# Attention rows kept as two half-precision planes, turned by transposing loads ahead of the output projection, in a hybrid decoder layer on one core

## The chip, the cores and the metric

One NeuronCore of one Trainium2 chip runs the whole kernel. The metric is device time of one execution in microseconds (us). The kernel before took 1151.21 us, median of 3 runs (1151.15 to 1152.17).

## The reference, cut to what matters

One decoder layer of width 1024 on a sequence of 2048 rows, batch 1, all inputs float32. `FOX` is causal softmax attention with a forget-gate bias (8 heads of 64), `SWA` is attention in a sliding window of 128 keys with rotary positions and a learned sink (8 query heads, 2 key/value heads).

```python
mod = silu(c) @ w_ada + b_ada                       # shift, scale, gate: 1024 each
h = rms_norm(x, g_pre) * (1 + scale) + shift
qa, ka, va, fa, za, qb, kb, vb, zb = split(h @ w_in)
oa = forgetting_attention(qa, ka, va, fa + b_fgate) * silu(za)      # [2048, 512]
ob = sliding_window_sink_attention(rope(qb), rope(kb), vb, sinks) * silu(zb)   # [2048, 512]
y = concatenate([oa, ob], axis=-1) @ w_out          # [2048, 1024] @ [1024, 1024]
out = x + gate * rms_norm(y, g_post)
```

## The kernel before, in words

**Numbers.** TensorE works on float16 pairs: a float32 value times a power of two is kept as a high part (a copy to float16) and a low part (value minus high part). A product of two such pairs is three float16 matmuls: high by high, high by low, low by high.

**Stages.** The work is one long program in a hand-written order for all engines (`tc.manual_schedule()`). First the input is normalised, turned and projected. Then come 32 `Pair` windows of the sliding-window attention, with projections filled in between (`fill`). Then comes the forgetting attention: 8 heads `hd`, each of 20 `Step`s `r` (two key blocks against a chunk `ci` of 512 queries, 4 chunks per head, with 2, 4, 6 and 8 steps). Last comes the output projection, class `Out`, one object for each of 16 tiles `t` of 128 rows. The first units of it are filled into the last head.

**Where attention rows go.** Both attentions write their divided results to DRAM, in `o_d`, four tensors of 512 rows by 1024 columns in float32. A window does it in `out_` (line 934): VectorE multiplies by the inverse sums into the tile `on`, and GpSimd's queue issues the store (line 938). A head's chunk does it at the end of `Step.pv` (line 1363): VectorE writes `ona`, and SyncE's queue (SP) issues the store (line 1368). The gates, silu paths already in transposed layout, are written to `z_d`, with the feature on the partition.

**The output projection, tile by tile.** `load_z` and `load_o` (lines 1454 and 1459) bring a tile's gates and its 128 rows of `o_d` into two buffers each, cut from `Ts[0]`. `turn` (line 1465) transposes the rows on TensorE: 8 float32 transposes of 128 by 128 against the identity (line 1469) into two PSUM banks. Later steps of it are put off by ticks (`after(n, f)` calls `f` at the n-th next `tick()`): `gate` multiplies the banks with the gates (line 1478, VectorE, twice 512 columns), `squares_` sums squares (1481, ScalarE), `scale_` adds over partitions with a matmul (1485) and makes a power-like scale, then the high part (1491, ScalarE) and the low part (1492, VectorE) go to the tile `oz`. `product(n, k)` (line 1494) issues three matmuls of 512 columns (line 1505) for feature block `k` and output half `n`; a tile has 16 such units, 48 matmuls. After the eighth unit `evac` squares the bank (1513, ScalarE) and multiplies by the gate vector (1521, VectorE). `root` is a chain of small VectorE operations (lines 1531 to 1552), and `store` (1555) adds the residual (1559, VectorE) and issues the output store on SP's queue (1560).

**Order.** `ofill` runs the units in order: tiles 0 and 1 interleaved, then tile after tile, with a `tick` every second unit. Tile t + 1 is turned after the third unit of tile t, with its scale 4 ticks later. In the last head (`hd == 7`) tiles 0 and 1 are loaded at steps 4 and 6 and turned at 6 and 8; the last 16 projection units lie in steps 0 to 7, and 33 units of the output projection in steps 10 to 19. `w_out_load` and `w_out_split` bring and split the output weights in the same head.

**Buffers.** `op_` (tags `tz`, `ona`) has two buffers in the forgetting attention, `onp` two. Gates' small tiles (`nn`, `cm`, `tot`) lie in the pool `fap`.

Of the kernel before, what the change touches and what calls it, by code (L numbers as in the profile page):

```python
# [18 lines left out]
P = 128  # L19
S = 2048  # L20
D = 1024
# [19 lines left out]
def hybrid_layer(  # L41
# [32 lines left out]

    o_d = [dram.tile([CH, D], F32, name=f"o_d{t}") for t in range(NCH)]
    z_d = dram.tile([KT, P, S], F32, name="z_d")
# [111 lines left out]
    def after(n, f):  # L188
        late.append([n, f])
# [610 lines left out]
    def gates():  # L800

        nn = fap.tile([P, 2, NB, 8], F32, tag="nn", name="nn")
        nf, na = nn[:, 0], nn[:, 1]
# [10 lines left out]
        def sums():  # L814
# [3 lines left out]
            PE.matmul(pc[:, P:2 * P], ones[:], lsf, start=True, stop=True)  # L818
            cm = fap.tile([P, 2, NB, 8], F32, tag="cm", name="cm")
            V.tensor_copy(cm[:].rearrange("p a t h -> p (a t h)"), pc[:, 0:2 * P])  # L820
# [5 lines left out]
            for r in (2, 3):  # L826
                V.tensor_tensor(inn[:, :, r, :], inn[:, :, r - 1, :], blk[:, :, r - 1, :], op=ALU.add)
            tot = fap.tile([P, 4, 8], F32, name="tot")
# [5 lines left out]
            V.tensor_tensor(csum[:].rearrange("p h t -> p t h"), cm[:, 0], na,  # L834
                            op=ALU.add)

        after(1, logs)
# [11 lines left out]
    class Pair:  # L849
# [73 lines left out]
        def pv(self):  # L923
# [10 lines left out]
            def out_():  # L934
                on = onp.tile([P, 2, P], F32, tag="on", name="on")
                V.tensor_tensor(on[:].rearrange("p e (h d) -> p (e h) d", h=2), po[:],
                                self.rinv[:].unsqueeze(2).broadcast_to([P, 4, 64]), op=ALU.mult)
                G.dma_start(o_d[i // 4][(i % 4) * P:(i % 4 + 2) * P, (4 + j) * P:(5 + j) * P]
                            .rearrange("(e p) c -> p e c", p=P), on[:])

# [164 lines left out]
    with swa_order:  # L1105
# [47 lines left out]
        windows[NW - 1].pv()  # L1153
        tick()
        tick()
        banded[0] = False
# [15 lines left out]
    foxl, foxo = ExitStack(), ExitStack()  # L1172
    op_ = foxl.enter_context(tc.tile_pool(name="opa", bufs=2, reuse_waits="tile"))
    stp = foxl.enter_context(tc.tile_pool(name="stpa", bufs=3, reuse_waits="tile"))
# [139 lines left out]
    class Step:  # L1314
# [35 lines left out]
        def pv(self):  # L1350
# [12 lines left out]
            if self.last:  # L1363
                rinv = sm(4, "a_ri")
                V.reciprocal(rinv[:], po[:, :, 64])
                on = op_.tile([P, 4, 64], F32, tag="ona", name="ona")
                V.tensor_tensor(on[:], po[:, :, 0:64], rinv[:].unsqueeze(2).broadcast_to([P, 4, 64]), op=ALU.mult)  # L1367
                SP.dma_start(o_d[self.ci][:, hd * 64:(hd + 1) * 64].rearrange("(u p) d -> p u d", p=P), on[:])

# [25 lines left out]
    def open_out():  # L1395
# [3 lines left out]
        wo = foxo.enter_context(tc.tile_pool(name="wo", bufs=1, reuse_waits="tile"))  # L1399
        op_ = foxo.enter_context(tc.tile_pool(name="opo", bufs=2, reuse_waits="tile"))  # L1400
        stp = foxo.enter_context(tc.tile_pool(name="stpo", bufs=4, reuse_waits="tile"))
# [14 lines left out]
        spare = hT[2][:].rearrange("p a k n -> p (a k n)")  # L1416
        oio["r"] = [spare[:, 2 * CH * n:2 * CH * (n + 1)].bitcast(F32) for n in range(6)]
        oio["j"] = [spare[:, CH * a:CH * b].bitcast(BF16) for a, b in ((12, 14), (14, 15), (15, 16))]
        rotate("x", oxy[:2])
# [22 lines left out]
    class Out:  # L1442


        def __init__(self, t):
            self.t = t
            self.last = t == NB - 1
            self.cuts = (0, CH, CH + 3 * P, D) if self.last else (0, CH, D)

        def load(self):  # L1450
            self.load_z()
            self.load_o()
# [12 lines left out]
        def turn(self, lag):  # L1465

            px = [bk[bank()][:].rearrange("p (k n) -> p k n", k=4) for _ in range(2)]
            for k in range(KT):
                PE.transpose(px[k // 4][:, k % 4, :], self.o[:, k * P:(k + 1) * P], ident[:])  # L1469
# [3 lines left out]
            gs = sm(1, "w_mx")  # L1473

            def gate():
                for h in range(2):
                    z = self.z[:, 4 * h:4 * h + 4, :]
                    V.tensor_tensor(z, px[h], z, op=ALU.mult)  # L1478

# [12 lines left out]
            after(lag + 2, lambda: V.scalar_tensor_tensor(lo, self.z, self.sc[:], hi, op0=ALU.mult, op1=ALU.subtract))  # L1492

        def product(self, n, k):
# [15 lines left out]
            def evac():  # L1510
                if n == 0:
                    self.y = oio["y"]()
                A.activation(oio["j"][1 + n % 2][:, :cc.stop - cc.start], py, AF.Square, accum_out=self.ss[:, n:n + 1])
                if self.last:
                    if n == 0:
# [47 lines left out]

    ounits, oloads = [], {}
    for t, n in [(0, 0), (1, 0), (0, 1), (1, 1)] + [(t, n) for t in range(2, NB) for n in range(len(outs[t].cuts) - 1)]:
        if n == 0 and t + 2 < NB:
            oloads[len(ounits)] = t + 2
        for q in range(KT):
            ounits.append(lambda t=t, n=n, q=q: outs[t].product(n, q))
            nxt = 2 if (t, n) == (0, 1) else t + 1 if n == 0 and 2 <= t < NB - 1 else None  # L1570
            if q == 2 and nxt:
                ounits.append(lambda nxt=nxt: outs[nxt].turn(4))
    opos = [0]
    N_IN = 4 * KT + 1

    def ofill(n, each=None):
        for _ in range(n):
            if opos[0] in oloads:
                outs[oloads[opos[0]]].load()
            ounits[opos[0]]()  # L1580
            opos[0] += 1
            if each:
                each()

    with tc.manual_schedule():
# [29 lines left out]
        for s, stp_ in enumerate(steps):  # L1615
# [116 lines left out]
```

## Time and profile before

| | |
|---|---|
| median of the runs | 1151.21 us |
| the profiled execution's own time | 1151.65 us |
| its span, first to last instruction | 1149.9 us |
| outside the span | 1.75 us |
| mean granted TensorE clock | 0.998 of full speed |
| busy: TensorE, VectorE, ScalarE, GpSimd | 97%, 79%, 59%, 15% of the span |
| DMA moved | 136.36 MB, 119 GB/s mean |
| `o_d` loads in the output projection | 16 of 512 KB |
| `o_d` stores | 64 of 128 KB, half by GpSimd's queue, half by SP's |

Engines: PE is TensorE's matmul, PEld its weight loads, DVE VectorE, ACT ScalarE, POOL GpSimd, SP SyncE. A name with a small q (SPq) is that engine's instruction queue: issue of DMAs and waits on semaphores. A row of the windows view has the stretch in us, its length, then the busy time of each engine with its count of instructions, then the granted clock, the mean busy share of the 16 DMA engines (it can pass 1, since packets of one engine overlap) and what they moved in GB/s. A row of the chain has start, duration, engine, tile and line. A row of the view of one line has engine, operation, count, then duration in ns as smallest/median/largest, and the first and last start.

### The profile page before, as it was taken

The numbers are of one execution on the slowest core, as the hardware profiler recorded it, in microseconds if no ns is written. First come the engines' busy times: TensorE is split into PE (matmuls) and PEld (weight loads), VectorE is DVE, ScalarE is ACT, GpSimd is POOL, SyncE is SP. The second block draws the span as 40 slices with busy tenths as digits, with TensorE's granted clock in tenths as the row PEclk, the third lists the DMA queues.
The fourth block names the chain that finished last, engine by engine and source line by source line (L and its number), as shares of the span: only waits on it lengthen the run. The fifth ranks groups of instructions, "written<-read, shape, count | busy, mean of one in ns | idle before, by whom it ended". The sixth has DMA issues, their size and how long they took to land. (4 is left out here: it accounts for less than half of the span.)

```text
span 1149.9 us, 27039 instructions
## 1 busy us (share of the span) xinstructions
PE 1112.5 (97%) x10514; PEld 650.9 (57%) x10514; DVE 907.7 (79%) x2330; ACT 678.4 (59%) x1124; POOL 169.5 (15%) x302
## 2 busy tenths in 40 slices
PE   5899999999999999999999999999999989999997
PEld 1466657655579865555555555555555555455553
DVE  6776668879888577889988989888898886766666
ACT  4676446556566525766767667667777698233331
POOL 2011122333322201112111111111010010000000
PEclk9999999999999999999999999999999999999999
DMA  9646426687777423333333232214121264464542
GB/s 327 225 139 170 106 70 139 112 170 139 176 143 128 97 61 84 81 86 74 84 81 97 64 86 68 62 38 100 45 56 34 66 195 145 163 207 166 201 169 88
DMA packets 162452, 136.36 MB, mean 119 GB/s; under 512 B 95356, under 2 KB 139428, under 8 KB 162324
## 3 DMA queue, kind: packets, MB, share of 16 engines
q1 hardware_dynamic: 152388, 106.39, 35.6%
q0 software_dynamic: 9456, 27.72, 9.0%
q8 instruction: 82, 1.34, 0.5%
q10 hardware_dynamic: 480, 0.53, 0.2%
q14 instruction: 46, 0.38, 0.1%
HBM read 70.97 MB, written 25.18 MB: 84 GB/s over the span
## 5 line engine op out<-in xcount | busy, mean ns | idle before, releaser
L1337 ACT ACTIVATE p<-sta,lift,scl_qk 128x1024 f32<-128x1024 f32 (+2 forms) x160 | 171.8, 1074 | 90.7 <-PE sta L1333 85.1
L335 PE MATMUL bk<-hT,wh_qk 128*128 128x512 f16 x768 | 197.8, 378 | 0.0
L1505 PE MATMUL bk<-wohl,oz 128*128 128x512 f16 (+2 forms) x792 | 172.5, 372 | 2.2 <-DVE oz L1492 1.0
L1348 DVE TENSOR_TENSOR pha<-p,pha 128x1024 f16<-128x1024 f32 (+2 forms) x160 | 169.5, 1059 | 0.0
L1345 ACT ACTIVATE pha<-p 128x1024 f16<-128x1024 f32 (+2 forms) x160 | 148.1, 925 | 33.5 <-POOL p L1341 29.7
L1286 DVE TENSOR_REDUCE a_m<-bk 128x1 f32<-128x512 f32 x192 | 129.3, 683 | 36.2 <-PE bk L1283 35.7
L1505 PEld LDWEIGHTS <-oz 128*128 128x128 f16 x792 | 75.8, 99 | 83.2 <-issue 1.8
L1358 PE MATMUL poa<-vt,pha 128*128 128x65 f16 x1088 | 116.6, 193 | 2.0 <-DVE ona L1367 2.0
L1361 PE MATMUL poa<-vt,pha 128*128 128x65 f16 x1088 | 116.0, 192 | 1.3 <-DVE pha L1348 1.3
L1360 PE MATMUL poa<-vt,pha 128*128 128x64 f16 x1088 | 116.4, 194 | 0.0
L1332 PE MATMUL sta<-T 128*128 128x512 f16 (+1 forms) x320 | 109.6, 348 | 3.4 <-ACT p L1337 3.4
L1358 PEld LDWEIGHTS <-pha 128*128 128x128 f16 x1088 | 101.7, 97 | 16.5 <-DVE ona L1367 3.0
L1283 PE MATMUL bk<-T 66*128 66x512 f16 (+2 forms) x320 | 110.5, 348 | 0.1
L335 PEld LDWEIGHTS <-wh_qk 128*128 128x128 f16 x768 | 70.1, 97 | 69.6 <-issue 0.6
L1360 PEld LDWEIGHTS <-pha 128*128 128x128 f16 x1088 | 101.1, 97 | 13.5
L1333 PE MATMUL sta<-T 69*128 69x512 f16 (+1 forms) x320 | 108.0, 348 | 0.0
L1361 PEld LDWEIGHTS <-pha 128*128 128x128 f16 x1088 | 100.8, 99 | 1.6 <-DVE pha L1348 1.6
L335 PE MATMUL bk<-hT,wh_za 128*128 128x512 f16 x384 | 99.9, 379 | 0.0
L1341 POOL TENSOR_SCALAR_AFFINE_SELECT p<-p 128x256 f32<-128x256 f32 x64 | 34.6, 541 | 415.8 <-ACT p L1337 411.0
L353 PE MATMUL bk<-wh_va,hT 128*128 128x128 f16 x1536 | 92.6, 219 | 0.0
L335 PE MATMUL bk<-hT,wh_zb 128*128 128x512 f16 x384 | 90.8, 379 | 0.0
L353 PEld LDWEIGHTS <-hT 128*128 128x128 f16 x1536 | 87.5, 98 | 4.9 <-issue 2.5
(497 smaller groups left out, 1849.6 us busy)
## 6 DMA issues: line engine op xcount, KB each, us to landing
hT<-in_x_dram SPq DMA_DIRECT2D x20, 512.0 KB
wa<-in_w_ada_dram SPq DMA_DIRECT2D x16, 512.0 KB
T<-stq SPq DMA_DIRECT2D x128, 64.0 KB
T<-z_d SPq DMA_DIRECT2D x16, 512.0 KB
T<-o_d SPq DMA_DIRECT2D x16, 512.0 KB
z_d<-tz POOLq DMA_DIRECT2D x30, 256.0 KB, 3.0
out_dram<-hT SPq DMA_DIRECT2D x15, 512.0 KB
xt<-in_x_dram SPq DMA_DIRECT2D x12, 512.0 KB
```

Of the source, the lines that this page charges most:

```text
L335: PE.matmul(ps, whl[:, a, k, :], hT[ci][:, b, k, :], start=(k == 0 and n == 0), stop=(k == KT - 1 and n == 2))
L353: PE.matmul(ps[:, u * P:(u + 1) * P], hT[ci][:, a, k, u * P:(u + 1) * P], whl[:, b, k, :], start=(k == 0 and n == 0), stop=(k == KT - 1 an ...
L1283: PE.matmul(mx[:, :w], T[0:XM, 0, i * P:(i + 1) * P], T[0:XM, 2, pc * CH:pc * CH + w], start=True, stop=True)
L1286: V.tensor_reduce(m3[:, u, pc:pc + 1], mx[:, :w], axis=AX.X, op=ALU.max)
L1332: PE.matmul(self.st[:, o:o + w], T[:, 3, kb_], T[:, 1, qc], start=True, stop=False)
L1337: A.activation(self.p32[:, :self.w], self.st[:, :self.w], AF.Exp, scale=scl[f"qk{self.hd}"][:], bias=lift[:])
L1345: A.activation(self.ph[:, 0, :self.w], self.p32[:, :self.w], AF.Copy)
L1348: V.tensor_tensor(self.ph[:, 1, :self.w], self.p32[:, :self.w], self.ph[:, 0, :self.w], op=ALU.subtract)
L1358: PE.matmul(po[:, u, :], ph[:, 0, pq], vt[:, b, hd, 0:65], start=(self.first and n == 0 and u == 0), stop=False)
L1360: PE.matmul(po[:, u, 0:64], ph[:, 0, pq], vt[:, b, hd, 65:VW], start=False, stop=False)
L1361: PE.matmul(po[:, u, :], ph[:, 1, pq], vt[:, b, hd, 0:65], start=False, stop=(self.last and n == len(self.blocks) - 1))
L1505: PE.matmul(py, self.hl[:, i, k, :], w_slot(8 * j + k)[:, cc], start=(k == 0 and m_ == 0), stop=(k == KT - 1 and m_ == 2))
```

## The change

`o_d` becomes float16 with twice the rows: each block of 128 rows is followed by its low parts, in the same bytes as before. Where rows are made, two operations and a later store take the place of the store:

```diff
@@ Pair.pv, out_
-                G.dma_start(o_d[i // 4][(i % 4) * P:(i % 4 + 2) * P, (4 + j) * P:(5 + j) * P]
-                            .rearrange("(e p) c -> p e c", p=P), on[:])
+                oh = onp.tile([P, 2, 2, P], F16, tag="oh", name="oh")
+                def put():
+                    rows_ = slice(2 * (i % 4) * P, 2 * (i % 4 + 2) * P)
+                    G.dma_start(o_d[i // 4][rows_, (4 + j) * P:(5 + j) * P].rearrange("(m p) c -> p m c", p=P),
+                                oh[:].rearrange("p e a c -> p (e a) c"))
+                after(1, lambda: A.activation(oh[:, :, 0], on[:], AF.Copy))
+                after(3, lambda: V.tensor_tensor(oh[:, :, 1], on[:], oh[:, :, 0], op=ALU.subtract))
+                after(4, put)
@@ Step.pv
-                SP.dma_start(o_d[self.ci][:, hd * 64:(hd + 1) * 64].rearrange("(u p) d -> p u d", p=P), on[:])
+                oh = op_.tile([P, 4, 2, 64], F16, tag="oha", name="oha")
+                def put():
+                    SP.dma_start(o_d[self.ci][:, hd * 64:(hd + 1) * 64].rearrange("(m p) d -> p m d", p=P),
+                                 oh[:].rearrange("p u a d -> p (u a) d"))
+                after(1, lambda: A.activation(oh[:, :, 0], on[:], AF.Copy))
+                after(2, lambda: V.tensor_tensor(oh[:, :, 1], on[:], oh[:, :, 0], op=ALU.subtract))
+                after(3, put)
```

The pool `op_` goes from two buffers to one in the forgetting attention and in the last head, so `tz`, `ona` and `oha` have one each. The gates' small tiles get a pool of their own that closes behind them. Three more ticks follow the last window.

In the output projection a tile's rows come by two transposing loads of 128 by 1024 float16 each, high and low plane, into the two buffers that held the float32 rows. VectorE adds the planes into a float32 tile `c` (one buffer), and one multiplication of 1024 columns gates it:

```diff
@@ Out
-            self.o = Ts[0][:, t % 2, :].bitcast(F32)
-            SP.dma_start(self.o, o_d[t // 4][(t % 4) * P:(t % 4 + 1) * P, :])
+            self.o = Ts[0][:, t % 2, :].rearrange("p (a k n) -> p a k n", a=2, k=KT)
+            for a in range(2):
+                SP.dma_start_transpose(self.o[:, a], o_d[t // 4][(2 * (t % 4) + a) * P:(2 * (t % 4) + a + 1) * P, :])
...
-            px = [bk[bank()][:].rearrange("p (k n) -> p k n", k=4) for _ in range(2)]
-            for k in range(KT):
-                PE.transpose(px[k // 4][:, k % 4, :], self.o[:, k * P:(k + 1) * P], ident[:])
...
+            def join():
+                V.tensor_tensor(c, self.o[:, 0], self.o[:, 1], op=ALU.add)
             def gate():
-                for h in range(2):
-                    z = self.z[:, 4 * h:4 * h + 4, :]
-                    V.tensor_tensor(z, px[h], z, op=ALU.mult)
+                V.tensor_tensor(self.z, c, self.z, op=ALU.mult)
...
-            after(1, gate)
-            after(2, squares_)
+            after(1, join)
+            after(2 if lag > 4 else 1, gate)
+            after(3 if lag > 4 else 2, squares_)
```

In `evac` the multiplication by the gate vector (line 1521, with the bank's release behind it) moves one tick later for all tiles but the last. Output stores go to GpSimd's queue, the last tile's excepted. The order is now written as three tables by unit: tile t (from 5) has its rows loaded at unit 16(t - 3) + 1, its gates at 16(t - 3) + 10, and is turned at 16(t - 2) + 6 with the scale 7 ticks later; a tile's own units begin at 16t.

```diff
-            for n, e in enumerate((SP, A) if self.last else (SP,)):
+            for n, e in enumerate((SP, A) if self.last else (G,)):
...
+    orows = {1: 2, 5: 3, 18: 4}
+    oloads = {0: 2, 8: 3, 30: 4}
+    oturns = {10: 2, 22: 3, 39: 4}
+    for t in range(5, NB):
+        orows[2 * KT * (t - 3) + 1] = t
+        oloads[2 * KT * (t - 3) + 10] = t
+        oturns[2 * KT * (t - 2) + 6] = t
...
-                npn = len(punits) - P_LAST + P_LAST * min(r + 1, 8) // 8 - pos[0]
-            if hd == 7 and r >= 8:
-                npn, fil = N_IN * max(r - 9, 0) // (NS - 10) - opos[0], ofill
+                npn = len(punits) - P_LAST + (2 * (r + 1) if r < 4 else 8 + min(8 * (r - 3) // 7, 8)) - pos[0]
+            if hd == 7 and r > 10:
+                npn, fil = N_IN * (r - 10) // (NS - 11) - opos[0], ofill
...
-            if hd == 7 and r in (4, 6):
-                outs[r // 2 - 2].load_o()
-            if hd == 7 and r in (6, 8):
-                outs[r // 2 - 3].turn(4)
+            if hd == 7 and r in (5, 6):
+                outs[r - 5].load_o()
+            if hd == 7 and r in (7, 9):
+                outs[(r - 7) // 2].turn(4)
```

In the last head the 16 projection units now reach to step 10, and 32 units of the output projection lie in steps 11 to 19.

More of the change, by code (lines that the diff above doesn't have):

```diff
@@ L73, in hybrid_layer @@
     small = ctx.enter_context(tc.tile_pool(name="small", bufs=4))
-    o_d = [dram.tile([CH, D], F32, name=f"o_d{t}") for t in range(NCH)]
+    o_d = [dram.tile([2 * CH, D], F16, name=f"o_d{t}") for t in range(NCH)]
     z_d = dram.tile([KT, P, S], F32, name="z_d")
@@ L835, in sums @@
                             op=ALU.add)
+            gtx.close()
         after(1, logs)
@@ L1153, in hybrid_layer @@
         windows[NW - 1].pv()
-        tick()
-        tick()
+        for _ in range(5):
+            tick()
         banded[0] = False
@@ L1562, in hybrid_layer @@
     outs = [Out(t) for t in range(NB)]
[L1564 to L1572, printed above, removed]
+    ounits = [(t, n, q) for t, n in [(0, 0), (1, 0), (0, 1), (1, 1)]
+              + [(t, n) for t in range(2, NB) for n in range(len(outs[t].cuts) - 1)] for q in range(KT)]
+    N_IN = 4 * KT
+    orows = {1: 2, 5: 3, 18: 4}
[5 more added lines that the diff above has]
+        oturns[2 * KT * (t - 2) + 6] = t
     opos = [0]
-    N_IN = 4 * KT + 1
     def ofill(n, each=None):
@@ L1578, in ofill @@
             if opos[0] in oloads:
-                outs[oloads[opos[0]]].load()
-            ounits[opos[0]]()
+                t = oloads[opos[0]]
+                assert outs[t - 2].turned
+                outs[t].load_z()
+            if opos[0] in orows:
+                t = orows[opos[0]]
+                assert outs[t - 2].joined
+                outs[t].load_o()
+            if opos[0] in oturns:
+                outs[oturns[opos[0]]].turn(7)
+            t, k, q = ounits[opos[0]]
+            assert outs[t].turned
+            outs[t].product(k, q)
             opos[0] += 1
```

29 lines of the change are left out of this document (20 added, 9 removed).

## The prediction, made before the changed kernel ran

> **What bounds the kernel now.** I read the page's busy shares first, then a table of stages, then the chain that ended last in order of time, then the engines' own timelines where the chain is quiet.
>
> ```profile
> span 1149.9 us, 27039 instructions
> PE 1112.5 (97%) x10514; PEld 650.9 (57%) x10514; DVE 907.7 (79%) x2330; ACT 678.4 (59%) x1124; POOL 169.5 (15%) x302
> ```
>
> TensorE is busy for 97% of the span, but an average hides where it is not. The windows view splits it: two stretches of attention, the end of the last head, and the output projection by itself.
>
> ```profile
> 200.00:300.00 100.00, 100.00 (x962) 54.78 (x960) 87.24 (x262) 61.16 (x155) 33.80 (x65) 1.00 0.73 147
> 500.00:600.00 100.00, 98.92 (x1012) 55.83 (x1010) 89.82 (x196) 69.76 (x93) 17.34 (x28) 1.00 0.31 77
> 928.00:997.00 69.00, 63.81 (x621) 37.11 (x620) 50.49 (x96) 48.18 (x66) 3.54 (x6) 1.00 0.51 163
> 997.00:1127.00 130.00, 130.00 (x667) 66.80 (x666) 88.59 (x271) 41.78 (x80) 0.00 (x0) 1.00 0.52 179
> ```
>
> The second number is the stretch, the third TensorE's busy time, the fifth VectorE's. From 997 to 1127 us TensorE never rests at the full granted clock (1.00), while VectorE is busy 68% and the DMA engines 52%. So in this stage an instruction taken from TensorE shortens the run by its own length. From 928 to 997 us it rests 5.19 us. In attention it is nearly full, but VectorE is at 87% and 90%, so operations added there have little room.
>
> The chain of work that ended last shows what repeats in the output projection:
>
> ```profile
> 997.50 0.87 PE bk L1469 x8
> ...
> 1054.35 0.87 PE bk L1469 x8
> 1055.22 3.88 PE bk L1505 x18
> 1059.22 6.50 PE bk L1505 x30
> 1065.72 0.87 PE bk L1469 x8
> ...
> 1122.57 0.87 PE bk L1469 x8
> 1127.44 14.99 PE bk L1505 x93
> ```
>
> One tile takes 1065.72 - 1054.35 = 11.37 us: 48 products of line 1505 (3.88 and 6.50), 0.12 for the scale, and 0.87 for eight transposes of line 1469. The turns are strictly on the chain.
>
> **What goes.** The view of line 1469 counts all of them:
>
> ```profile
> L1469 PE MATMUL bk<-ident,T x128: 272/273/304, 933.6 to 1123.2; 128*128 128x128 f32 x128
> ```
>
> and TensorE's timeline has the turn of tile 3 ahead of the chain's first (a bracket at a row's end would tell of rest before it):
>
> ```profile
> 985.29 1.04 PE L1469 MATMUL bk<-ident,T 128*128 128x128 f32 x8
> ```
>
> That is 16 turns. From 997.50 to 1122.57 there are (1122.57 - 997.50) / 11.37 = 11 periods, so 12 turns, and tile 3's starts at 985 us with no rest ahead of it. So 13 turns stand where TensorE alone sets the pace: 13 x 0.87 = 11.3 us. A tile then takes 11.37 - 0.87 = 10.50 us, if nothing else is later. The other 3 turns, 2.6 us, lie in the last head.
>
> **Whether VectorE keeps up with 10.50 us.** Its timeline of one tile:
>
> ```profile
> 1077.56 1.29 DVE L1478 TENSOR_TENSOR T<-bk,T 128x512 f32<-128x512 f32 x2 [0.91 <-PE bk L1469]
> 1078.77 0.15 DVE L1531 TENSOR_TENSOR w_sw<-w_pw,ysc 128x1 f32<-128x1 f32 x1
> ...
> 1082.00 0.16 DVE L112 TENSOR_SCALAR sc_h<-bk 128x1 int32<-128x1 int32 x1 [0.36 <-PE bk L1485]
> ...
> 1082.28 0.69 DVE L1521 TENSOR_TENSOR hT<-bk,gacc 128x512 f32<-128x512 f32 x1
> 1082.88 1.27 DVE L1559 SCALAR_TENSOR_TENSOR hT<-hT,y_rs 128x1024 f32<-128x1024 f32 x1
> 1084.08 1.28 DVE L1492 SCALAR_TENSOR_TENSOR oz<-T,w_pw,oz 128x1024 f16<-128x1024 f32 x1
> ```
>
> From start to start: gating 1078.77 - 1077.56 = 1.21; the root chain up to the wait, 1082.00 - 0.36 - 1078.77 = 2.87; the scale 0.28; two of line 1521, 0.60 each; the residual 1.20; the low part 1.28. In all 8.04 us of 11.37. The change takes the 1.21 away and adds a join and a gating of 1024 columns, neither of which is in this trace. The nearest row is the low part of attention, also two inputs of 1024 columns in SBUF with a float16 among them:
>
> ```profile
> L1348 DVE TENSOR_TENSOR pha<-p,pha 128x1024 f16<-128x1024 f32 (+2 forms) x160 | 169.5, 1059 | 0.0
> ```
>
> At 1.06 each VectorE has 8.04 - 1.21 + 2.12 = 8.95 us in 10.50. Bounds for one: 0.60 (line 1521's 512 columns) and 1.28 (line 1492), so 8.0 to 9.4. I take 1.06, the same operation at the same size. 1.5 us remain, and the deferred gate multiply, the later scale and the earlier turn only move work inside the tile: by the tables the low part is queued about 8 units before the tile's first product, 8 x 0.65 = 5.2 us (a unit is three of the 48 products' 10.38 us). So this is costed at nothing; without that cover it costs what exceeds 10.50, times 13.
>
> **Whether the loads keep up.** The kernel already issues transposing loads in the windows, from SBUF, also 128 by 1024 in float16. No trace here shows one that reads DRAM. Their issue on SP's queue, and the DMA engines around two of them with a store beside:
>
> ```profile
> L910 SPq DMA_TRANSPOSE ptb<-sp x32: 1211/1256/2547, 166.5 to 381.0; - x32
> 367.16 1.96 SPq L910 DMA_TRANSPOSE ptb<-sp  x1
> 369.18 1.30 SPq L915 DMA_TRANSPOSE ptb<-sp  x1
> 366.62 0.71 POOL L938 DMA_DIRECT2D o_d<-on  x1 [4.28 <-DVE on L936]
> 367.00:368.00 1.00, 1.00 (x22) 1.00 (x20) 0.96 (x3) 0.14 (x1) 0.34 (x2) 1.00 0.22 61
> 368.00:369.00 1.00, 1.00 (x20) 0.85 (x19) 0.90 (x2) 0.00 (x0) 0.65 (x2) 1.00 1.24 191
> 369.00:370.00 1.00, 1.00 (x20) 0.79 (x17) 0.56 (x3) 0.00 (x0) 0.25 (x2) 1.00 0.91 29
> 370.00:371.00 1.00, 1.00 (x22) 1.00 (x20) 0.96 (x4) 0.85 (x2) 0.00 (x0) 1.00 1.11 176
> 371.00:372.00 1.00, 1.00 (x23) 1.00 (x21) 0.94 (x6) 0.97 (x5) 0.00 (x0) 1.00 1.02 215
> 372.00:373.00 1.00, 1.00 (x33) 1.00 (x31) 0.89 (x6) 0.97 (x4) 0.00 (x0) 1.00 0.00 0
> ```
>
> The shares add to 4.50 us of all 16 engines. In the output projection four transfers of 512 KB make 0.52 x 11.37 = 5.91 us a tile, 1.48 each, so a store of 128 KB is 0.37. Two transposing loads are then 4.13, one 2.07 us. The new tile needs 3 x 1.48 + 4.13 = 8.57 us of 10.50: 82%, high but not the bound. On SP's queue two issues of 1.26 us and two plain loads fit well, and the output store's wait for VectorE leaves that queue, so the loads behind it start earlier. On GpSimd's queue nothing is queued behind the stores in this stage (busy 0.00 from 997 on). The rows are asked for at unit 16(t - 3) + 1 and used past unit 16(t - 2) + 6, 21 units or 13.7 us later, against two issues and 4.13 us. So I price the loads at nothing: not below, because TensorE does not wait for DMA there now, and above by the rival below.
>
> A rule speaks against the change: the Trainium skill, "VectorE: DVE Perf Modes", section "The three transpose paths", gives 390 ns for a 128 by 128 turn on TensorE and 1309 ns by DMA, and the page's rules for authors prefer TensorE where PSUM is a fine destination. By it 16 blocks per tile would take an estimated 21 us of DMA, and the stage would be slower; the trace has 2.07 us for eight blocks and 0.87 us for TensorE's eight, so it agrees on the order of the two and not on the size.
>
> **What is added in attention.** Sixty-four copies to float16 on ScalarE and 64 subtractions on VectorE, 256 columns each, 32 in each attention:
>
> ```profile
> L1367 DVE TENSOR_TENSOR ona<-poa,a_ri x32: 423/424/425, 453.9 to 983.8; 128x256 f32<-128x256 f32 x32
> L1186 ACT ACTIVATE wsq<-wsq 128x256 f32<-128x256 f32 x32 | 12.8, 401 | 0.0
> L938 POOL DMA_DIRECT2D o_d<-on x32: 706/726/797, 180.9 to 395.9; - x32
> DMA to landing us min/median/max: 2.2/2.7/5.1
> ```
>
> By the nearest rows of 256 columns 0.42 and 0.40 us. In the windows 32 x 0.42 = 13.4 us over the 216 us from 180 to 396: VectorE goes from 87% to 93%. In the forgetting attention 13.4 over 530 us: from 90% to 92%. Behind each subtraction wait the bank evacuations on VectorE and, behind those, TensorE's next units; behind the store on GpSimd's queue the rotary multiply, but the store is put a tick behind the subtraction. With one buffer, a chunk's copy on ScalarE must also wait until the store of the chunk before has left. From the last chunk of a head to the first of the next that is two steps, 6.6 us (a head is 66 us), two of whose four ticks go by ahead of the store; 3.3 us remain against a landing of 2.7, so it just fits. Bounds: 0, if all hides, to 13, half of VectorE's 27 on the path. I take 1.5, near the lower end, because VectorE stays below full on average.
>
> **The last head.** It loses 2.6 us of TensorE but TensorE rests there anyway:
>
> ```profile
> PE poa L1361 <- DVE pha L1348: 1.3, 2, 1.1
> PE sta L1332 <- ACT p L1337: 1.2, 2, 0.8
> PE bk L1505 <- DVE oz L1492: 1.0, 1, 1.0
> PE bk L1505 <- ACT wohl L1439: 0.8, 1, 0.8
> ```
>
> These are TensorE's waits from 890 to 1005 us: several engines bind by turns. I count half of the 2.6, a gain of 1.3. Bounds: a gain of 7.8 (2.6 and all 5.19 of rest) and a loss of 3, if the first join waits on VectorE for the store's 2.7 us and its two loads.
>
> The tail behind the last product keeps its operations. Sum: -11.3 + 1.5 - 1.3 = -11.1 us. The profiled execution took 1151.65 us (span 1149.9 and 1.75 outside), 0.44 above the median of 1151.21; on the median that gives 1140.1.
>
> **Rivals.**
> - VectorE eats part of it: added operations in attention, or a join of 1.28 and waits within a tile, make it late in places. For it: 87 to 90% busy and in order. Against: averages below 94%. At 4 to 8 us given back: 1143 to 1148.
> - Transposing loads bind, on the slower side. If a load from DRAM costs T on all engines, a tile needs 4.44 + 2T. It passes TensorE's 10.50 at T = 3.03, and the old 11.37 at T = 3.47. At twice the SBUF row, 4.14, a tile takes 12.7 us: 13 x 1.35 = 18 us more, 1167. Against: the row's 2.07; for it: no row reads DRAM. The rule of the Trainium skill above is this case.
> - The turns' time is not won, since a new wait as long takes their place (the single tile `c`, the one output buffer): within 0.2% of 1151. Against: 1.5 us of room per tile on VectorE.
> - More: the last head's rests close as well, 1132 to 1136.5.
>
> **How the numbers follow.** Forecast (1136.5 to 1143) 0.72; VectorE 0.12; no gain 0.05; loads bind 0.07; more 0.04. The predicted time is the forecast's own. The range leaves out the last three and a little of the second: 1136 to 1147. Faster by over 0.2% (2.3 us, about what a measurement of this kernel can tell) is 0.72 + 0.12 + 0.04 = 0.88, same 0.05, slower 0.07.
>
> **What would show it.** Line 1469 gone from the chain; the tile's period 10.5 us with TensorE busy throughout; join and gating near 1.06 us each; VectorE at about 85% and DMA at about 80% of the stage. The forecast is wrong if TensorE waits for `oz` in the output projection, if VectorE's join waits for the loads, or if TensorE's rest in attention grows by more than 3 us.

## The result, and the profile after

The changed kernel takes **1162.61 us**, median of 5 runs (1161.09 to 1163.94), against 1151.31 us for the kernel before beside it (5 runs, 1151.15 to 1152.17): a ratio of 1.0095, 95% interval 1.008 to 1.011. It is slower by 11 us, where 11 us less was forecast. The profiled execution took 1161.38 us.

First the page of the changed kernel, its span and busy shares:

```profile
span 1159.6 us, 26925 instructions
PE 1106.1 (95%) x10386; PEld 638.6 (55%) x10386; DVE 949.7 (82%) x2394; ACT 694.1 (60%) x1188; POOL 174.7 (15%) x317
```

TensorE's busy time fell by 1112.5 - 1106.1 = 6.4 us, though 16 turns of 0.87 us, 13.9 us, went: what is left took longer (the last section has one reason). The sum of work doesn't say where the time went. The views of single lines give markers in both kernels: the last product of the windows, the first score of the forgetting attention, the reduction with which the last head begins, and the last attention product. Behind the colon stand the smallest, median and largest duration in ns, then the first and the last start in us. Before:

```profile
L930 PE MATMUL pob<-vb,ptb x744: 192/193/193, 178.0 to 395.0; 128*128 128x64 f16 x186
L1332 PE MATMUL sta<-T x320: 219/379/390, 433.3 to 975.9; 128*128 128x512 f16 x128, 128*128 128x256 f16 x32
L1424 DVE TENSOR_REDUCE w_p<-fac x1: 149/149/149, 916.2 to 916.2; 128x1 f32<-128x8 f32 x1
L1361 PE MATMUL poa<-vt,pha x1088: 191/192/205, 449.5 to 983.3; 128*128 128x65 f16 x182
```

and the same four lines of the changed kernel:

```profile
L933 PE MATMUL pob<-vb,ptb x744: 189/193/203, 177.7 to 409.2; 128*128 128x64 f16 x186
L1343 PE MATMUL sta<-T x320: 219/379/631, 447.8 to 997.4; 128*128 128x512 f16 x128, 128*128 128x256 f16 x32
L1444 DVE TENSOR_REDUCE w_p<-fac x1: 151/151/151, 932.6 to 932.6; 128x1 f32<-128x8 f32 x1
L1372 PE MATMUL poa<-vt,pha x1088: 191/192/247, 464.0 to 1004.9; 128*128 128x65 f16 x182
```

| stretch | before, us | after, us | difference |
|---|---|---|---|
| start to first score | 433.3 | 447.8 | +14.5 (of it +14.2 by the last window product) |
| first score to last head | 482.9 | 484.8 | +1.9 |
| last head to last attention product | 67.1 | 72.3 | +5.2 |
| from there to the end of the span | 166.6 | 154.7 | -11.9 |

The four differences add to +9.7 us, the difference of the spans; the medians differ by 11.3, since the profiled execution of the changed kernel lies 1.2 us under its median. The output projection gained what was forecast; the stages that make the rows gave more than that away. In the output projection the chain that ended last now has no transposes:

```profile
1018.40 10.38 PE bk L1530 x48
1028.90 10.38 PE bk L1530 x48
```

A period is 1028.90 - 1018.40 = 10.50 us, the forecast number; the last such row starts at 1123.37 us, ten periods after the first. The windows view of this stage and VectorE's timeline of one tile:

```profile
1010.00:1130.00 120.00, 120.00 (x573) 56.21 (x572) 100.19 (x267) 39.87 (x79) 5.85 (x11) 1.00 0.77 196
```

```profile
1064.68 1.22 DVE L1493 TENSOR_TENSOR osum<-T 128x1024 f32<-128x1024 f16 x1
1065.93 1.23 DVE L1497 TENSOR_TENSOR T<-osum,T 128x1024 f32<-128x1024 f32 x1
```

TensorE is busy for all 120 us, VectorE for 83%, the DMA engines for 77%, and no bracket stands at the join or the gate: VectorE does not wait here. The view of line 1493 names no wait at any of the 16 joins of this execution, so nothing waits for the transposing loads. All the rest of this document is on the other three stretches.

### The profile page after: what moved, and what is told of

It reads as the page before. It is cut to its first block, busy times and chain, and to the rows that moved or that the text cites. A ratio compares the mean times of both kernels' runs of the same rounds, so it can differ in the third digit from the quotient of the medians.

```text
span 1159.6 us, 26925 instructions
## 1 busy us (share of the span) xinstructions
PE 1106.1 (95%) x10386; PEld 638.6 (55%) x10386; DVE 949.7 (82%) x2394; ACT 694.1 (60%) x1188; POOL 174.7 (15%) x317
## 4 chain that ended last, share of the span: by engine, by line
PE 54%; DVE 22%; issue 4%; ACT 4%; DMA 1%; POOL 0%; DVEq 0%; ACTq 0%; POOLq 0%
PE bk L335 18%; PE bk L1530 14%; PE sta L1343 4%; PE sta L1344 4%; PE bk L1294 4%; DVE sp L917 3%; PE poa L1371 2%; PE poa L1372 2%; PE poa L1369 2%; ACT sp L912 2%; DVE a_m L1297 2%; PE bk L353 2%; DVE pha L1359 1%; DVE wmx L230 1%; DVE b_nb L887 1%
## 5 line engine op out<-in xcount | busy, mean ns | idle before, releaser
L1530 PE MATMUL bk<-wohl,oz 128*128 128x512 f16 (+2 forms) x792 | 169.4, 372 | 0.8 <-DVE oz L1514 0.8
L1352 POOL TENSOR_SCALAR_AFFINE_SELECT p<-p 128x256 f32<-128x256 f32 x64 | 31.6, 494 | 424.8 <-ACT p L1348 412.3
L335 PE MATMUL bk<-hT,wh_qb 128*128 128x512 f16 x384 | 91.1, 385 | 4.4 <-DVE wh_qb L279 4.4
```

The source lines that it names most:

```text
L335: PE.matmul(ps, whl[:, a, k, :], hT[ci][:, b, k, :], start=(k == 0 and n == 0), stop=(k == KT - 1 and n == 2))
L1530: PE.matmul(py, self.hl[:, i, k, :], w_slot(8 * j + k)[:, cc], start=(k == 0 and m_ == 0), stop=(k == KT - 1 and m_ == 2))
```

## Experiments on the windows

**What the trace shows there.** ScalarE's timeline of the changed kernel, around one window; a bracket is the rest before the instruction, with what ended it:

```profile
228.59 0.42 ACT L948 ACTIVATE oh<-on 128x256 f16<-128x256 f32 x1 [1.00 <-DVE on L939]
228.91 0.92 ACT L912 ACTIVATE sp<-sm__3076 128x256 f16<-128x256 f32 x2
...
233.35 0.51 ACT L895 ACTIVATE sm__3197<-sm__3197,b_nb 128x257 f32<-128x257 f32 x1 [3.04 <-DVE b_nb L887]
```

and VectorE's and TensorE's beside it:

```profile
228.14 0.41 DVE L939 TENSOR_TENSOR on<-pob,b_ri 128x256 f32<-128x256 f32 x1
229.34 2.12 DVE L917 TENSOR_TENSOR sp<-sm__3076,sp 128x256 f16<-128x256 f32 x2 [0.79 <-ACT sp L912]
...
234.29 0.74 DVE L279 SCALAR_TENSOR_TENSOR wh_qb<-wr_qb,w_sw,wh_qb 128x512 f16<-128x512 f32 x1
```

```profile
235.09 1.89 PE L335 MATMUL bk<-hT,wh_qb 128*128 128x512 f16 x4 [3.89 <-DVE wh_qb L279]
```

Read them as a loop. The copy of the finished window (line 948) stands on ScalarE's queue ahead of the high part of the window two further on (912), and both are due in the same tick. The copy cannot start before VectorE has made the quotient `on` (939), at the end of its own queue of work. So the high part, whose own input is ready, starts late; the low part on VectorE (917) waits for it; the maxima of the next window come behind the low part, its exponentials (895) behind those. The probabilities `sm_` have one buffer, so no window gets ahead. The split of the projection weights (279) is queued on VectorE in the same loop, and at 235 us TensorE has rested 3.89 us for it. The view of waits counts it over the stage (180 to 410 us; us in all, times, longest), changed kernel and then the kernel before:

```profile
ACT oh L948 <- DVE on L939: 23.9, 26, 2.2
DVE sp L917 <- ACT sp L912: 26.7, 22, 1.4
```

```profile
DVE sp L914 <- ACT sp L909: 14.5, 14, 2.9
```

The rival is load: 64 operations more on two engines in a stage where VectorE was busy 87%.

**Copy one tick later.** Only the place in the queue changes; the same work is done.

```diff
@@ Pair.pv, out_ of the changed kernel
-                after(1, lambda: A.activation(oh[:, :, 0], on[:], AF.Copy))
+                after(2, lambda: A.activation(oh[:, :, 0], on[:], AF.Copy))
```

> The changed kernel, but in the windows ScalarE's copy to float16 comes one tick later, behind the window's own high part; subtraction and store stay where they are. Theory Q (the copy waits on ScalarE for VectorE's quotient, with the softmax loop's high part queued behind it, and so makes the windows' loop longer than TensorE's work): most of the 14.2 us that the windows lost come back, so about 1149 to 1152, and the last window's products end near 397 us instead of 409. Theory L (the windows are bound by VectorE's added subtraction): no gain, 1161 to 1163.

Measured: 1146.55 us (1146.5 to 1147.0), ratio to the kernel before 0.9957 (0.9943 to 0.9972). The line takes 16.1 us off the changed kernel by the medians, and in the profiled executions the windows end 14.7 us earlier: not most of the 14.2 us, as theory Q had it, but all. The stretch of 200 to 300 us in the changed kernel, and then this one's last window product and the same stretch (TensorE's busy time third, VectorE's fifth, granted clock third from the end):

```profile
200.00:300.00 100.00, 93.31 (x876) 49.96 (x874) 85.61 (x252) 60.12 (x156) 29.25 (x56) 0.97 0.62 126
```

```profile
L933 PE MATMUL pob<-vb,ptb x744: 192/193/193, 177.4 to 394.5; 128*128 128x64 f16 x186
```

```profile
200.00:300.00 100.00, 100.00 (x955) 54.49 (x953) 93.09 (x277) 66.06 (x172) 34.13 (x64) 1.00 0.77 147
```

The windows end at 394.5 us, half a microsecond earlier than before the change. VectorE is now busy 93%, as the prediction's sum said, and TensorE does not rest from 200 to 300 us. In the changed kernel VectorE was busy 86%: it had more room there, not less.

**One operation at a time, on the kernel before.** The copy alone, then the subtraction alone, each into a scratch tile that nothing reads (the low part in the second is `on` minus itself; what goes to DRAM is as before). The gates' small tiles have their own pool in both, to make room.

```diff
@@ Pair.pv, out_ of the kernel before, first kernel
+                oh = onp.tile([P, 2, P], F16, tag="oh", name="oh", bufs=1)
+                after(1, lambda: A.activation(oh[:], on[:], AF.Copy))
@@ second kernel
+                oh = onp.tile([P, 2, P], F16, tag="oh", name="oh", bufs=1)
+                after(3, lambda: V.tensor_tensor(oh[:], on[:], on[:], op=ALU.subtract))
```

> The kernel before, with one part of the change alone: in the windows ScalarE copies the quotient to float16 in a scratch tile one tick behind it (with the gates' small tiles in their own pool for room). Output unchanged. Theory Q: the windows lose most of what they lost in the changed kernel, 9 to 14 us, so 1160 to 1165. Theory L: nothing, 1151 to 1152.5.

> The kernel before, with the other part alone: in the windows VectorE makes one subtraction of 256 columns into a scratch tile three ticks behind the quotient. Theory Q: little, 1151 to 1154. Theory L: 9 to 14 us more, 1160 to 1165.

Measured: the copy 1157.02 us (1156.62 to 1159.99), ratio 1.0053 (1.0038 to 1.0068); the subtraction 1151.82 us (1151.51 to 1157.03), ratio 1.0009 (0.9999 to 1.0019). Last window product and stretch of 200 to 300 us, of the copy first and then of the subtraction:

```profile
L933 PE MATMUL pob<-vb,ptb x744: 189/193/193, 177.9 to 400.3; 128*128 128x64 f16 x186
```

```profile
200.00:300.00 100.00, 96.97 (x908) 52.09 (x906) 85.16 (x248) 61.02 (x163) 29.47 (x58) 0.98 0.66 132
```

```profile
L933 PE MATMUL pob<-vb,ptb x744: 192/193/203, 177.6 to 396.0; 128*128 128x64 f16 x186
```

```profile
200.00:300.00 100.00, 100.00 (x957) 54.56 (x955) 93.67 (x279) 61.89 (x159) 32.59 (x64) 1.00 0.77 147
```

The added load of VectorE is harmless (93.67% busy, no rest of TensorE); the copy on the emptier engine, ScalarE, costs 5.3 us of the windows by itself, less than the 9 to 14 that theory Q expected. Load by itself is out. The change costs 14.2, more than 5.3 + 1.0. That the subtraction weighs more once the loop is late would fit, since it stands in the same loop, but this is argued: neither kernel has both operations or the change's later store, and the excess of 7.9 was not taken apart. The later copy wins it back as well, with subtraction and store in place.

## Experiments on the last head

The view of waits of the changed kernel from 917 to 1005 us, and a row of its chain that ended last:

```profile
ACT oha L1385 <- DMA o_d<-oha: 3.0, 1, 3.0
SPq L1454 <- DMA z_d<-tz: 10.6, 1, 10.6
PE sta L1343 <- ACT p L1348: 7.3, 4, 2.9
```

```profile
941.51 5.17 DMA o_d<-oha
```

Three suspects: the one buffer `oha` (a copy on ScalarE waits 3.0 us until a store has landed, which takes 5.17); the first weight loads on SP's queue, which wait 10.6 us for the store of the last gates out of the one `tz`, since the weights' landing tile lies over its place; and the first tile's join, whose transposing loads wait 2.2 us on SP's queue for the chunk's store (VectorE itself has no wait at the join in this execution).

**Two buffers `oha`**, alone and with the later copy in the windows:

```diff
@@ Step.pv of the changed kernel
-                oh = op_.tile([P, 4, 2, 64], F16, tag="oha", name="oha")
+                oh = op_.tile([P, 4, 2, 64], F16, tag="oha", name="oha", bufs=2)
```

> The changed kernel with two buffers for the float16 rows of the forgetting attention, where it has one. Theory S (in the last head a chunk's copy waits 3.0 us on ScalarE for the store of the chunk before, and the softmax behind it): 3 to 5 us back, 1157.5 to 1159.5, and no wait of ScalarE for that store. Rival (the last head is slow because the first rows arrive late through the transposing loads): within 1 us of 1162.6.

> The changed kernel with the windows' copy one tick later and two buffers for the float16 rows of the forgetting attention: the two edits that each gave time alone (16.1 and 2.6 us). If the two losses are apart, they add: 1143.5 to 1145. Rival (the last head is bound by its late weights and rows as well, so a second buffer gains nothing once the windows are mended): 1146 to 1147.

Measured: alone 1160.05 us (1159.15 to 1161.88), ratio 1.0076 (1.0061 to 1.0091), 2.6 below the changed kernel; with the later copy 1145.1 us (1144.49 to 1145.9), ratio 0.9945 (0.993 to 0.996), 1.4 below the later copy alone. The wait of `oha` for its store is gone from ScalarE's waits. The intervals of the ratios overlap in both comparisons, but the markers of the profiled executions agree: the last head is 70.7 us long for 72.3 without the later copy, and 71.1 for 72.8 with it. So the one buffer costs some 1.6 us there.

**The first weights.** Two kernels try to free them. One gives `tz` two buffers in the heads ahead of the last (pool `opa` with `bufs=2`, `ona` kept at one, `oha` at one there and at two in the last head, the later copy in). The other keeps the kernel of before this paragraph (later copy, two `oha`) and opens the weights' pool ahead of the smaller one in `open_out`, so that its first tile lands elsewhere:

```diff
@@ open_out
+        stp = foxo.enter_context(tc.tile_pool(name="stpo", bufs=4, reuse_waits="tile"))
         op_ = foxo.enter_context(tc.tile_pool(name="opo", bufs=1, reuse_waits="tile"))
-        stp = foxo.enter_context(tc.tile_pool(name="stpo", bufs=4, reuse_waits="tile"))
```

> The kernel with both edits (two buffers for the float16 rows in the last head alone) and with two buffers again for the gate tile of the forgetting attention. Theory B (in the changed kernel the first loads of output weights wait 10.6 us on SP's queue for the last store of the one gate tile, whose memory they take over, and ScalarE then waits 1.9 us for them): the wait shrinks to some 4 us, and 1 to 2.5 us are won against both edits alone. Rival: the weights are not on the path, no difference beyond 0.5 us.

> The kernel with the windows' copy later and two buffers for the float16 rows, and in the last head the pool of the weights' landing tiles is opened ahead of the pool of the rows, so that the first landing tile no longer lies over the gate tile, whose last store it waited 10.7 us for on SP's queue. Theory W (ScalarE's and VectorE's 2.0 us wait for the first weights pushes the last head back, TensorE's clock falls behind it): 1 to 3 us faster than 1145.1, and the first weights land before their split. Rival (the wait only moves to the second landing tile or to the rows): within 0.7 us of 1145.1.

Measured: two `tz` 1145.08 us (1144.95 to 1146.71), ratio 0.9947 (0.9933 to 0.9962); SP's queue still waits 10.4 us, so it tells nothing of what that wait costs. Weights' pool first: **1143.63 us** (1143.12 to 1144.29), ratio 0.9931 (0.9917 to 0.9946), the fastest kernel of the study, 1.5 below the kernel it edits (the intervals overlap; no run of one reaches the runs of the other). ScalarE's wait for the weights (2.0 us for `wo` in that kernel) is gone; SP's queue, the kernel that is edited and then this one, shows the loads of the weights (a row takes several issues together, with a wait between them):

```profile
920.83 1.36 SPq L1454 DMA_DIRECT2D wo<-in_w_out_dram  x3
```

```profile
909.82 11.21 SPq L1454 DMA_DIRECT2D wo<-in_w_out_dram  x3
```

The first load now goes out 11 us earlier; a later one still waits 9.6 us for the store of the gates. Gone with ScalarE's wait are a rest of TensorE of 2.19 us, up to 926.6 us in the kernel that is edited, and the stretch behind it with the granted clock at 0.50 (927.5 to 930.8 us). The markers of this kernel are

```profile
L1444 DVE TENSOR_REDUCE w_p<-fac x1: 152/152/152, 917.8 to 917.8; 128x1 f32<-128x8 f32 x1
L1372 PE MATMUL poa<-vt,pha x1088: 191/192/247, 449.2 to 986.9; 128*128 128x65 f16 x182
```

a last head of 69.1 us, where 71.1 was in the kernel it edits and 67.1 before the change.

**The first join.** What is left in that fastest kernel is seen on the timelines of VectorE, ScalarE and TensorE, and in a stretch of the windows view:

```profile
940.00 1.23 DVE L1493 TENSOR_TENSOR osum<-T 128x1024 f32<-128x1024 f16 x1 [1.27 <-DMA T<-o_d]
941.26 1.22 DVE L1497 TENSOR_TENSOR T<-osum,T 128x1024 f32<-128x1024 f32 x1
942.52 1.06 ACT L1500 ACTIVATE hT<-T 128x1024 bf16<-128x1024 f32 x1 [1.65 <-DVE T L1497]
943.57 1.19 ACT L1348 ACTIVATE p<-sta,lift,scl_qk 128x1024 f32<-128x1024 f32 x1
944.81 0.38 PE L1343 MATMUL sta<-T 128*128 128x512 f16 x1 [3.34 <-ACT p L1348]
```

```profile
946.00:948.00 2.00, 2.00 (x26) 1.44 (x24) 1.93 (x4) 2.00 (x3) 0.71 (x1) 0.50 0.96 248
```

It is the pattern of the windows again: the join waits for the load, the gate for the join, ScalarE's squares for the gate, and the exponential that TensorE needs stands behind the squares. Putting the squares a tick later (`turn(5)` in place of `turn(4)` in the last head, where a lag over 4 also puts gate and squares a tick later) was tried on the kernel with the later copy and two `oha`, and then with the weights' pool first:

```diff
-                outs[(r - 7) // 2].turn(4)
+                outs[(r - 7) // 2].turn(5)
```

> The kernel with both edits, and the two turns in the last head use a lag of 5 instead of 4: gating one tick behind the join, squares two ticks behind it, scale at the fifth. Theory J (ScalarE's squares wait for the join and the gating, which wait for the transposing loads, with the step's exponential queued behind them, and TensorE rests 3.2 us): that rest goes, 2 to 4 us faster than 1145.1. Rival (the first product comes too soon behind the later scale): TensorE waits 1 to 3 us for the low part of the first tile instead, no gain.

> Both mends of the last head together. If the two waits are apart, their gains add: 1139 to 1142, the time that was predicted for the change. If the last head is simply full on ScalarE, no better than the better one alone.

Measured: 1146.04 us (1145.77 to 1147.01), ratio 0.9954 (0.9937 to 0.997), and 1143.89 us (1143.55 to 1144.71), ratio 0.9934 (0.992 to 0.9949): 0.9 and 0.3 above the kernels without the edit. The waits of the kernel with the later copy and two `oha`, and then of the first of these two, say why:

```profile
PE sta L1343 <- ACT p L1348: 7.4, 5, 3.2
```

```profile
PE sta L1343 <- ACT p L1348: 5.8, 6, 2.0
PE bk L1504 <- ACT hT L1500: 2.0, 1, 2.0
```

The longest wait for the exponential fell from 3.2 to 2.0 us, and TensorE then waited 2.0 us for the squares themselves at the scale's matmul (line 1504). The expected gain moved into a new wait, as the rival said, though at another place than the rival named.

## Experiments on the heads before it

Between the first score and the last head the change costs 1.9 us. TensorE's rest from 432 to 916 us before and 448 to 932 us after is 3.3 and 4.7 us. Three kernels look for the cause. The first moves copy, subtraction and store of a chunk a tick later each, on the kernel with the later copy and two `oha`. The second does that on the kernel with two `tz`. The third, on the fastest kernel, puts the 28 subtractions of heads 0 to 6 on GpSimd, and their stores a tick later.

```diff
@@ Step.pv, first and second
-                after(1, lambda: A.activation(oh[:, :, 0], on[:], AF.Copy))
-                after(2, lambda: V.tensor_tensor(oh[:, :, 1], on[:], oh[:, :, 0], op=ALU.subtract))
-                after(3, put)
+                after(2, lambda: A.activation(oh[:, :, 0], on[:], AF.Copy))
+                after(3, lambda: V.tensor_tensor(oh[:, :, 1], on[:], oh[:, :, 0], op=ALU.subtract))
+                after(4, put)
@@ Step.pv, third
-                after(2, lambda: V.tensor_tensor(oh[:, :, 1], on[:], oh[:, :, 0], op=ALU.subtract))
-                after(3, put)
+                after(2, lambda: (G if hd < 7 else V).tensor_tensor(oh[:, :, 1], on[:], oh[:, :, 0], op=ALU.subtract))
+                after(3 if hd == 7 else 4, put)
```

> The kernel with both edits, and in the forgetting attention too the copy, the subtraction and the store come one tick later, so that the copy stands behind the step's high part on ScalarE. Theory Q also for these heads (the copy waited 20.0 us in 16 places for VectorE's quotient in the changed kernel): 0.5 to 2 us faster than with both edits alone. Rival (those waits lie in ScalarE's rest): no difference beyond 0.5 us, or slower in the last head, whose first rows then leave a tick later.

> All edits together: windows' copy later, two buffers for rows in the last head, two for the gate tile, copy, subtraction and store a tick later in the forgetting attention. If all of them stand, the sum: 1140 to 1143, about what the prediction of 1140.1 left out of the attention stages; if the last head is bound otherwise, 1144 to 1146.

> The kernel with the windows' copy a tick later, two buffers oha and the weights' pool opened first (1143.63 us), with the forgetting attention's subtractions of heads 0 to 6 on GpSimd in place of VectorE, and their stores a tick later; the last head as it was. Theory L (VectorE's 28 added subtractions of 0.42 us, 11.8 us of work on an engine that is busy 87%, are what the heads 0 to 6 lose): from the first score of the forgetting attention to the start of the last head it takes 482.9 us again, as before the change, in place of 484.8, and the run 1141.7 us. Theory S (the copies on ScalarE, which stand ahead of exponentials there, are the price): 484.8 stays, 1143.6. Rival G (GpSimd's work slows VectorE's rows beside it): VectorE's low parts pha get longer than 1.06 us on average, and the run is above 1145 us.

Measured: 1145.38 us (1144.35 to 1147.12), ratio 0.9948 (0.9933 to 0.9963), level with 1145.1; 1150.1 us (1145.52 to 1151.32), ratio 0.9983 (0.9972 to 0.9993), with a spread that was not explained, so nothing is built on it; and 1145.52 us (1144.8 to 1145.61), ratio 0.9943 (0.9929 to 0.9956), 1.9 slower than the kernel it edits.

In these heads the copy's place costs nothing. ScalarE waited 16.9 us in 14 places ahead of the copy in the kernel with two `oha`; with the later copy it waits 3.8 us in 4 and the heads take as long (484.7 us), so those waits lay in ScalarE's own rest. GpSimd's subtraction is slower by itself (a median of 672 ns), and the heads took 486.4 us (434.2 to 920.6) in place of 484.8. (The first window product of that execution already starts 1.2 us late, which the edit does not touch.) But the run did not take the load off VectorE. These are the heads in the windows view, the fastest kernel and then this one:

```profile
433.00:917.80 484.80, 480.12 (x4768) 268.79 (x4766) 425.08 (x955) 339.12 (x463) 64.35 (x115) 1.00 0.29 70
434.20:920.60 486.40, 480.22 (x4768) 268.80 (x4766) 424.06 (x928) 339.32 (x463) 88.10 (x142) 1.00 0.29 70
```

VectorE has 27 instructions fewer, some 11 us of work, and is busy only 1.0 us less: others of its instructions became longer beside GpSimd's (the 29 of line 1311 took 7.6 us in all for 5.5). Its low parts, in groups by line from 433 to 917 us, were 1077 ns on average beside it and 1060 without (this kernel, then the fastest), as rival G forecast:

```profile
L1359 DVE TENSOR_TENSOR pha<-p,pha 128x1024 f16<-128x1024 f32 (+2 forms) x139 | 149.7, 1077 | 0.0
```

```profile
L1359 DVE TENSOR_TENSOR pha<-p,pha 128x1024 f16<-128x1024 f32 (+2 forms) x140 | 148.4, 1060 | 0.0
```

So theory L was not put to its test, and the 1.9 us stay open. What speaks for VectorE's load is argued from waits alone: from first score to last head TensorE's wait for the quotients `ona` is 1.8 us in the changed kernel for 1.1 before, and a wait of 0.3 for low parts is new.

## Why the prediction was wrong, point by point

- **The turns (right).** Forecast: 13 turns on the chain, a period of 10.50 us, 11.3 us gained. Measured: 10.50 us, and 11.9 us from the last attention product to the end.
- **VectorE and the loads in the output projection (right, one size off).** Join and gate took 1.22 and 1.23 us for the 1.06 taken, inside the bounds given; VectorE 83% for 85%; DMA 77% for 80%. The rival that transposing loads from DRAM bind there did not come about: TensorE was busy for all 120 us. (By its own terms that rival comes to 1169 us, not 1167; nothing hangs on it.) The Trainium skill's price for a turn by DMA, 1309 ns (page "VectorE: DVE Perf Modes", section "The three transpose paths"), made an estimated 21 us a tile; it does not hold for these loads, since a tile's two, with three other transfers beside them, fit in 10.50 us.
- **What is added in attention (the step that failed).** It was priced at 1.5 us, with bounds of 0 and 13, from VectorE's average load. Windows and heads 0 to 6 lost 14.5 + 1.9 = 16.4 us, outside the bounds. The step asked how full the engines were and named what is queued behind the subtraction; it never asked what is queued behind the *copy* on ScalarE. That was the high part, on the loop that sets the windows' pace. The later copy gave the 14 us back with the same work, and the subtraction alone cost nothing that can be measured. The upper bound was wrong in kind: it took half the duration of VectorE's added operations for the most that the step can cost and left ScalarE's copies out, but the copy's waits alone came to 23.9 us, and they hold up what is queued behind them. The prediction's own sign of failure came: TensorE's rest in the windows grew by 9.9 us, where 3 was the limit that it named.
- **The rival "VectorE eats part of it" (wrong mechanism).** It gave 4 to 8 us back, by load. The time was lost by order, on the engine that had room.
- **One buffer in the heads (failed, small).** "3.3 us remain against a landing of 2.7, so it just fits": the landing was the median of the windows' stores, whose own row reaches 5.1. The store that mattered took 5.17 us, and the copy was due 2.2 us behind its issue (946.7 less the wait of 3.0, less 941.5), so it waited 3.0. It cost some 1.6 us, in the last head alone; in the heads before it the copy never waited for a store.
- **The last head (wrong sign).** Forecast a gain of 1.3, with bounds of 7.8 gained and 3 lost; it lost 5.2. The bound had the first join in it, but not the weights that wait for the gates' last store in a reused place (1.5 us by the edit of one pool's order), nor the buffer. Of it 2.0 us stay: TensorE waits 3.34 us behind the first join, and moving the squares did not win it.

Once the order and the buffer are mended the time comes near the forecast, 1143.63 us for 1140.1. In the fastest kernel the output projection gains 11.7 us for 11.3; windows and heads cost 1.6 for 1.5, which is luck, since the 1.5 was chosen between wide bounds for a kernel with another order; and the last head loses 2.0 where it was to gain 1.3, which is nearly all of the gap.

## What to carry to other kernels

Before adding a cheap operation to an in-order engine, list what it waits for, and what stands behind it on that queue; if one of those lies on a single-buffered loop, its wait can come back in every turn of the loop, whatever the engine's load (here 23.9 us of waits, 14.2 us lost). Let such an operation be issued behind the loop's own work: here one tick, with no work changed, decided between 11 us slower and 5 us faster. And when a pool loses a buffer, look at what else will be laid over its place and must wait for it.

## What the hardware showed that was not expected

**A rest of TensorE costs more than its length.** The windows view of the changed kernel in steps of 2 us, around the rest of 3.89 us that ended at 235.09:

```profile
232.00:234.00 2.00, 0.00 (x0) 0.00 (x0) 1.97 (x9) 0.65 (x3) 0.00 (x0) 0.82 0.55 105
234.00:236.00 2.00, 0.91 (x3) 0.37 (x4) 1.97 (x7) 1.54 (x6) 0.00 (x0) 0.50 0.00 0
236.00:238.00 2.00, 2.00 (x15) 0.79 (x13) 1.30 (x4) 0.63 (x2) 0.79 (x1) 0.50 0.40 91
238.00:240.00 2.00, 2.00 (x9) 0.60 (x6) 1.24 (x3) 1.82 (x3) 0.00 (x0) 0.50 0.41 112
240.00:242.00 2.00, 2.00 (x18) 1.05 (x16) 1.97 (x8) 0.00 (x0) 1.43 (x2) 0.98 1.02 195
```

The granted clock fell to 0.50 while TensorE still rested, 2.2 us into the rest (at 233.4 us by the same view in steps of 0.25 us), and stayed there to 240.1 us: half of the 4.91 us of work from 235.09 to 240 us, 2.5 us, was lost on top of the rest. The same is to be seen in the last head of the fastest kernel after a rest of 3.34 us (0.50 from 946 to 948 us, above); there the low stretch goes from 945.7 to 949.1 us, so it began only after the work had. It came with shorter rests too: 2.56 us in the windows of the kernel with the copy alone (to 231.76 us), and 1.97 us in the last head of the changed kernel (to 962.85 us, the clock at 0.50 from 963.7 us). In the kernel before, whose rests from 180 to 410 us are at most 1.1 us, the clock is 1.00 there throughout. In the windows of the changed kernel TensorE's rest grew by 9.9 us (10.6 from 180 to 410 us, against 0.7 from 180 to 396 before), and with the 2.5 us of clock that makes 12.4 of the 14.2 lost. The Trainium skill, "TensorE: Matmul & The Clock Gate", section "Part 1: The HAM clock gate (the "warmup" mystery)", has the clock halved after an idle window of about 3.4 us and full again after about 3.4 us of sustained work. The rests of 1.97 and 2.56 us differ from the first, and here the measurement decides; for the second, the clock was back 4.3 us after the work began again in the fastest kernel and 5.0 us after in the windows above.

**A store of 128 KB landed in 5.17 us where 2.7 was reckoned with.** Its runs are shorter than those of the windows' stores before (128 bytes for 512) and it goes by another queue. But the longest of those stores took 5.1 us as well, so the length of the runs need not be the cause; no run took it apart from what else the DMA engines moved at the time.
